# A two-layer attention, mLSTM and HGRN2 block: projections and output tiles beside the mLSTM released in quarters at every step of the recurrence

## The chip, the cores and the metric

The kernel runs on one core of a Trainium2 chip. A core has TensorE (PE in the profile, with PEld for its weight loads), VectorE (DVE), ScalarE (ACT), GpSimd (POOL) and SyncE (SP), which issues most DMAs; POOL issues the others. Each engine takes its own instructions in order and waits on semaphores for the others. The metric is the device time of one execution in microseconds (us), lower is better.

## The reference

1024 latent tokens and 256 context tokens of width 1024 pass through two layers. Layer 0 runs neighbourhood attention (16 heads) and a bidirectional mLSTM (4 heads of width 256) side by side, from one input projection to one output projection. Layer 1 has bidirectional HGRN2 heads. Cut to what matters here:

```python
def _ab_mixer(h_lat, h_ctx, w_in, ...):
    qa, ka, va, za, qb, kb, vb, ob, zb, g = _split_cols(h @ w_in, AB_SIZES)
    oa = neighbourhood_attention(qa, ka, va, ...)        # and context attention
    hb = mlstm forward + mlstm backward (qb, kb, vb, gates)
    hb = _rms(hb * sigmoid(ob), h_norm)
    ya, yb = oa * silu(za), hb * silu(zb)
    return concatenate([ya, yb]) @ w_out

def step(carry, xs):                # one chunk of the mLSTM, per head and direction
    C, n, m = carry
    s = (q k^T) * exp(dmat - m_t)
    num = s v + carry_w * q C ;  den = sum(s) + carry_w * q n
    h = num / max(|den|, exp(-m_t))
    C = dec * C + kw^T v ;       n = dec * n + sum(kw)
```

The output projection of layer 0 is a sum of two halves: `ya @ w_out[:1024]`, which needs the attention alone, and `yb @ w_out[1024:]`, which needs the mLSTM.

## The kernel before

All values are float32. Dense products split each operand into a rounded high part and the rest (`split`, L72 to L75: an ACT cast and a DVE subtraction) and sum three products, hi·hi, hi·lo and lo·hi, so one block of a projection is three matmuls (L127 to L129) and one block of the output projection is three matmuls (L745 to L747).

The token axis is cut into NT = 10 tiles of 128. The mLSTM works on chunks of 128 in both directions. `ml_all` (L424) runs its four heads staggered by five steps: at step g, head h works on its chunk i = g - 5h, where that is 0 to 9, so steps g = 0 to 4 have one head, 5 to 19 two heads and 20 to 24 one head. For each head and each of two directions `ml_rec` (L454) builds a decay matrix on DVE and ACT, multiplies it with the scores to SD (L466), and runs on TensorE the matmul with SD (the SD matmul, L468), two with the carried state C (L478) and two for the update of C (L485), with the C update on DVE (L493). Chunks of q, k and v are loaded one step ahead by SP (`ml_load`, L389, and L421 for q and k), transposed on TensorE (L400, L406) and multiplied to scores (L413). When both directions of a chunk are done, `ml_out` (L516) gates it with the o and z projections (L521 to L528, the root on POOL L152 and L154), transposes it (L532) and stores it. A float32 matmul on these unsplit operands shows as two records of the trace (L468, L478, L485, L413); a transpose shows as one.

Beside the recurrence the kernel has other work for TensorE, here called the filler. It consists of

- the v, o and z projections of head 3 (`ml_ahead`, L307, through `proj_out`, L269): each loads four weight blocks by SP, splits them, and makes five tiles of two token tiles by 256 columns, 48 matmuls each, 256 wide, followed by an eviction on ACT or ACT and DVE and a store from POOL;
- the first half of the output projection (`out_some`, L751): for each of two column blocks b = 1 and b = 0 of 512 columns, eight weight blocks are loaded and split, and for each of the ten token tiles two pieces of the attention's output are loaded (L732) and split (yh, yl), 24 matmuls 512 wide are summed, and the sum is copied by ACT (L756), to the accumulator in SBUF for b = 1 and through POOL's queue to DRAM for b = 0.

The filler's PSUM tiles are in the two banks of the tag "mm". The recurrence uses "tr" (two banks), "s" (two) and "acc" (two), not "mm". After the recurrence the second half of the output projection (`out_tile`, with weights `w2`) uses "mm" again.

The order of instructions on each engine is fixed when the program is built. A planner hands out instructions by priority along a planned timeline; of those that are ready in its plan, the one traced earlier goes first. `filler()` (L300) moves what is traced in it behind everything else by a million places, so the filler runs only where the recurrence has nothing ready in the plan. `issue_after(at)` adds an edge from the matmul `at` to each matmul traced in the block, so none of them stands before `at` in TensorE's order; loads, splits and evictions on other engines get no such edge. Which filler may run from which step is written out by hand in two tables:

```python
ML_AHEAD = {-1: ("v", 3), 1: ("o", 3), 4: ("z", 3)}
ML_OUT = {1: (8, 8, 9, 9, 10, 10, 11, 11, 12, 12), 0: (13, 14, 14, 15, 16, 17, 18, 20, 22, 24)}
```

v of head 3 goes in before the recurrence, behind a matmul of the attention; o after step 1, z after step 4; output tiles of block 1 two at a time after steps 8 to 12, those of block 0 after steps 13 to 24. The edge starts at the last SD matmul of that step. At step 7 the split input (`hh`, `hl`, all that the projections read) is released and the pool "oy" opens in its place, with the accumulator and seven of the slots for output weights; the other four are the projections' weight slots.

Of the kernel before, what the change touches and what calls it, by code (L numbers as in the profile page):

```python
# [9 lines left out]
F32 = mybir.dt.float32  # L10
# [8 lines left out]
P = 128  # L19
D = 1024  # L20
KD = D // P
# [25 lines left out]
class Prog:  # L47
# [81 lines left out]
            mm(ps, lhsT=ll(k), rhs=rh(k), start=False, stop=(last and k == nk - 1))  # L129


    def proj_nat(self, ps, w, tt, c0, n):
        hh, hl = self.hh, self.hl
        s = slice(tt * P, (tt + 1) * P)
        self.dense(
            ps, lambda k: hh[:, k, s], lambda k: hl[:, k, s],
            lambda k: w.h(k)[:, c0 : c0 + n], lambda k: w.l(k)[:, c0 : c0 + n], KD,
        )


# [122 lines left out]


    def na_values(self, b):
        self.proj_out(2 * D + b * 256, self.vd[:, b * 256 : (b + 1) * 256])
# [38 lines left out]


    def ml_ahead(self, part, h, rev=False):  # L307
        c0 = (4 + "qkvoz".index(part)) * D + h * 256
        gate = {"o": self.gate_o, "z": self.gate_z, "q": self.gate_q}.get(part)
        dst = self.md[(part, h)] = self.md_all[len(self.md)]  # L310
        self.proj_out(c0, dst, gate, rev)


    def ml_gates(self, pool, keep):
# [109 lines left out]
    def ml_all(self, pool):  # L424
# [20 lines left out]
        for g in range(5 * 3 + NT):  # L445
            for h in range(4):
                scores = load(h, g + 1 - 5 * h) if 0 <= g + 1 - 5 * h < NT else []
                if 0 <= g - 5 * h < NT:
                    at = self.ml_rec(h, g - 5 * h, seqs, st[h], pool)
                for score in scores:  # L450
                    score()
            yield g, at

    def ml_rec(self, h, i, seqs, st, pool):  # L454
        nc = self.nc
        C, hs = st["C"], st["hs"]
        for d in range(2):
            c = seqs[d][i]
            lastc = P - 1 if d == 0 else 0
# [8 lines left out]
            at = nc.tensor.matmul(num, lhsT=SD, rhs=st["v"][c], start=True, stop=(i == 0))  # L468
            if i > 0 or i < NT - 1:
                cw = self.t(pool, [P, P], F32, "mcw", 4)  # L470
                nc.scalar.activation(cw, Gb, AF.Exp, scale=-1.0, bias=self.mpb[:, d, h, i : i + 1])
# [36 lines left out]
            else:  # L508
# [4 lines left out]
        return at  # L513


    def ml_out(self, h, tt, hs, pool):  # L516
# [219 lines left out]
        return yh, yl  # L736


    def out_sum(self, ps, w, tt, qs, ysrc, yp, bufs, ys=None, rp=None):
        mm = self.nc.tensor.matmul  # L740
        for q in qs:
            yh, yl = ys[q] if ys else self.out_y(tt, q, ysrc, yp, bufs, rp)
            for k in range(8):
                kk = (q - qs[0]) * 8 + k
                mm(ps, lhsT=yh[:, k, :], rhs=w.h(kk), start=(kk == 0), stop=False)  # L745
                mm(ps, lhsT=yh[:, k, :], rhs=w.l(kk), start=False, stop=False)  # L746
                mm(ps, lhsT=yl[:, k, :], rhs=w.h(kk), start=False, stop=(kk == 8 * len(qs) - 1))  # L747
# [462 lines left out]
    def build(self):  # L1210
# [3 lines left out]
        with ExitStack() as es:  # L1214
# [107 lines left out]
                    if p2 < 7:  # L1322
                        z = self.na_z(p2 + 1, pool)
            with tc.tile_pool(name="ml", bufs=2) as pool, self.pp.phase(s=2, acc=2):
                wq, self.six = {}, [(self.wp, "w", 4)] * 4
                with self.filler(), tc.issue_after(self.at[8]):
                    self.ml_ahead(*ML_AHEAD[-1])
                self.mask = self.t(pool, [P, 2, P], F32, "mmask", 1)
                dma(out=self.mask, in_=a["mmask"])

                def wo(q, b, ring=None):
                    if not ring:
                        ring, self.six = self.six[:8], self.six[8:] + self.six[:8]
                    src = a["woab"][q * D : (q + 1) * D, b * 512 : b * 512 + 512]
                    return self.wblock(None, "wo", [src], 8, 512, ring=ring)

                for g, at in self.ml_all(pool):
                    with self.filler(), tc.issue_after(at.ins):
                        if g in ML_AHEAD:
                            self.ml_ahead(*ML_AHEAD[g])  # L1340
                        if g == 7:
                            rh.close()
                            wr, self.ogb = es.enter_context(ExitStack()), 1
                            yp = wr.enter_context(tc.tile_pool(name="oy", bufs=1, side="right"))
                            acc = self.t(yp, [P, NT, 512], F32, "oacc", 1)
                            self.six = self.six + [(yp, "wo", 7)] * 7
# [50 lines left out]
            with l1:  # L1397
# [44 lines left out]
                raw = [pool, 3, "wraw"]  # L1442
                for i, b in enumerate((1, 0)):
                    w = wo(0, b, (ring * 2)[8 * i : 8 * i + 8], raw)
                    self.out_some(w, 0, range(8), self.yd2, yp, acc if b else None, self.part)
# [156 lines left out]
```

## Time and profile before

| | us |
|---|---|
| three runs | 3517.46, 3510.55, 3509.28 |
| median of the runs | 3510.55 |
| the profiled execution, its own time | 3510.13 |
| its span in the profile | 3508.3 |
| 1341 to 1761 in the span (the mLSTM stage, about): TensorE busy | 408.75 of 420 |
| 1761 to 1841 (rest of the output projection): TensorE busy | 78.16 of 80 |

The mean granted clock of TensorE over the execution is 0.995. In rows with several engines, "(x...)" is the number of records that lie in the stretch. A row of a group has the line of the kernel, the engine, the operation, what it writes and reads, its shape and count, then the busy time in us, the mean length of one in ns, and the idle time of the engine just before them with what ended it. In rows of waits, "A <- B" says that A waited and B ended the wait.

### The profile page before, as it was taken

Reading aid. Unit: us, or ns where it says so; the run is one execution under the profiler, and the core shown is the slowest. Engines: PE = TensorE matmul, PEld = TensorE weight load, DVE = VectorE, ACT = ScalarE, POOL = GpSimd, SP = SyncE. Lnnn points to the kernel's source line nnn. Section 1 sums busy time; section 2 is a strip of 40 time slices with the busy share of each in tenths; the row PEclk is TensorE's granted clock in tenths of the full one; section 3 lists DMA queues with packets and bytes.
Section 4 is the critical chain, followed back from the end, with each engine's and each line's share of the span. In section 5 each row is a group of like instructions: output and inputs, shape, how many; then the busy total and the mean of one; then the engine's idle time right before and its main releaser. Section 6 shows DMA issues by size and latency. Waiting matters only on the chain. (4 is left out here: it accounts for less than half of the span.)

```text
span 3508.3 us, 64938 instructions
## 1 busy us (share of the span) xinstructions
PE 3453.9 (98%) x24438; PEld 3146.4 (90%) x24438; DVE 2374.5 (68%) x6009; ACT 1602.3 (46%) x3700; POOL 526.2 (15%) x844
## 2 busy tenths in 40 slices
PE   8999999999999999999999999999999999999999
PEld 5889999999999999988778999989999999999887
DVE  4668856766666654666767766577777767777855
ACT  5532135555445534555547333344444444444442
POOL 3211121222212211211211111000100000010010
PEclk9999999999999999999999999999999999999999
DMA  7552332332323235364484222211211221121346
GB/s 237 168 160 88 115 90 58 91 87 68 84 77 83 83 88 160 121 183 145 124 258 143 100 103 103 82 37 56 61 48 49 61 61 49 52 64 49 116 146 204
DMA packets 374409, 363.91 MB, mean 104 GB/s; under 512 B 30296, under 2 KB 323096, under 8 KB 373968
## 3 DMA queue, kind: packets, MB, share of 16 engines
q1 hardware_dynamic: 330096, 250.34, 24.4%
q0 software_dynamic: 44000, 109.42, 9.1%
q8 instruction: 193, 3.16, 0.4%
q14 instruction: 120, 0.98, 0.1%
HBM read 276.09 MB, written 83.42 MB: 102 GB/s over the span
## 5 line engine op out<-in xcount | busy, mean ns | idle before, releaser
L127 PE MATMUL mm<-wh,hh 128*128 128x256 f32 x2256 | 649.0, 288 | 4.6 <-DVE ev L922 2.7
L128 PE MATMUL mm<-wl,hh 128*128 128x256 f32 x2256 | 649.0, 288 | 1.9 <-DVE wl L75 1.8
L129 PE MATMUL mm<-wh,hl 128*128 128x256 f32 x2256 | 648.5, 288 | 0.0
L129 PE MATMUL mm<-hh,wl 128*128 128x512 f32 (+1 forms) x1344 | 491.5, 366 | 0.0
L127 PE MATMUL mm<-hh,wh 128*128 128x512 f32 (+1 forms) x1344 | 485.1, 361 | 0.0
L128 PE MATMUL mm<-hl,wh 128*128 128x512 f32 (+1 forms) x1344 | 483.6, 360 | 0.0
L127 PEld LDWEIGHTS mm<-wh,hh 128*128 128x128 f32 x2256 | 431.4, 191 | 12.7 <-issue 6.9
L128 PEld LDWEIGHTS mm<-wl,hh 128*128 128x128 f32 x2256 | 431.6, 191 | 7.2 <-DVE wl L75 2.7
L129 PEld LDWEIGHTS mm<-wh,hl 128*128 128x128 f32 x2256 | 431.1, 191 | 3.6 <-issue 0.7
L74 ACT CAST wh<-wraw 128x512 fp32r<-128x512 f32 x290 | 178.2, 620 | 263.1 <-PE mm L128 130.7
L128 PEld LDWEIGHTS mm<-hl,wh 128*128 128x128 f32 x1344 | 254.0, 189 | 32.0
L129 PEld LDWEIGHTS mm<-hh,wl 128*128 128x128 f32 x1344 | 253.9, 189 | 30.5 <-issue 0.2
L127 PEld LDWEIGHTS mm<-hh,wh 128*128 128x128 f32 x1344 | 254.3, 189 | 29.3
L1109 ACT COPY gksel<-gK 128x512 f32<-128x512 f32 x224 | 147.1, 663 | 218.9 <-PE s L1118 197.6
L75 DVE TENSOR_TENSOR wl<-wraw,wh 128x512 fp32r<-128x512 f32 x290 | 196.5, 686 | 51.9 <-ACT wh L74 49.4
L1118 PE MATMUL s<-gQ,gksel 128*128 128x128 f32 x1536 | 199.9, 276 | 0.0
L1118 PEld LDWEIGHTS s<-gQ,gksel 128*128 128x128 f32 x1536 | 192.4, 191 | 6.9
L745 PE MATMUL mm<-woh,yh 128*128 128x512 f32 x412 | 166.7, 405 | 6.7 <-ACT yh L74 6.5
L747 PE MATMUL mm<-woh,yl 128*128 128x512 f32 x412 | 165.3, 402 | 0.5 <-DVE yl L75 0.5
L746 PE MATMUL mm<-wol,yh 128*128 128x512 f32 x412 | 164.0, 399 | 0.0
L74 ACT CAST wh<-b 128x512 fp32r<-128x512 f32 x124 | 77.0, 622 | 187.1 <-PE sa L129 85.3
L1139 DVE TENSOR_TENSOR gQ<-gQ,gT 128x256 f32<-128x256 f32 x384 | 143.2, 414 | 26.1 <-PE s L1118 26.0
(456 smaller groups left out, 8491.9 us busy)
## 6 DMA issues: line engine op xcount, KB each, us to landing
wraw<-yd SPq DMA_DIRECT2D x144, 256.0 KB
wraw<-in_wc_dram SPq DMA_DIRECT2D x128, 256.0 KB
wraw<-in_wab_dram SPq DMA_DIRECT2D x98, 256.0 KB
md<-ev POOLq DMA_DIRECT2D x94, 256.0 KB, 2.8
adar<-in_wada_dram POOLq DMA_DIRECT2D x32, 512.0 KB, 4.9
b<-in_wc_dram SPq DMA_DIRECT2D x64, 256.0 KB
vzd<-qo POOLq DMA_DIRECT2D x56, 256.0 KB, 2.5
adar<-in_wada_dram SPq DMA_DIRECT2D x16, 512.0 KB
```

What stands on the lines that cost most here:

```text
L74: nc.scalar.copy(hi, x)
L75: nc.vector.tensor_tensor(out=lo, in0=x, in1=hi.bitcast(F32), op=ALU.subtract)
L127: mm(ps, lhsT=lh(k), rhs=rh(k), start=(first and k == 0), stop=False)
L128: mm(ps, lhsT=lh(k), rhs=rl(k), start=False, stop=False)
L129: mm(ps, lhsT=ll(k), rhs=rh(k), start=False, stop=(last and k == nk - 1))
L745: mm(ps, lhsT=yh[:, k, :], rhs=w.h(kk), start=(kk == 0), stop=False)
L746: mm(ps, lhsT=yh[:, k, :], rhs=w.l(kk), start=False, stop=False)
L747: mm(ps, lhsT=yl[:, k, :], rhs=w.h(kk), start=False, stop=(kk == 8 * len(qs) - 1))
L1109: nc.scalar.copy(ksel.rearrange("p (b s i) -> p b s i", s=2, i=h), pick(K))
L1118: nc.tensor.matmul(pa[:, c, :].rearrange("p (b s i) -> p b s i", s=2, i=h), lhsT=ksel[:, c * P : (c + 1) * P], rhs=qp[:, c * nbc : (c + 1) ...
L1139: nc.vector.tensor_tensor(out=t[:, i, :, s, :], in0=t[:, i, :, s, :], in1=bc(tot), op=ALU.mult)
```

## The change

The two tables go. `proj_out` and `out_some` become generators that stop after each quarter of a tile: 12 matmuls of a projection tile's 48, or 6 of an output tile's 24; the eviction and the store go with the last quarter. The o and z projections of head 3 and the twenty output tiles form one sequence, `beside()`, of 40 + 80 quarters. `ml_all` now yields after each head of each step, with a rate and its two SD matmuls (one for each direction). For each SD matmul the rate is added to a count, and as many whole quarters as the count holds are taken from the sequence, as filler with an edge from that SD matmul. The rate is 2.0 in steps with one head and 1.4 in steps with two, so the calls offer 20 x 2.0 + 60 x 1.4 = 124 quarters. The release of `hh` and `hl` and the opening of "oy" follow the last quarter of z, wherever that falls. v of head 3 stays where it was. Other users of the two helpers run the generators to their end at once.

```diff
-ML_AHEAD = {-1: ("v", 3), 1: ("o", 3), 4: ("z", 3)}
 ML_ORDER = [8, 9, 4, 5, 6, 7, 0, 1, 2, 3]
-ML_OUT = {1: (8, 8, 9, 9, 10, 10, 11, 11, 12, 12), 0: (13, 14, 14, 15, 16, 17, 18, 20, 22, 24)}
+ML_RATE = (2.0, 1.4)
...
     def proj_out(self, c0, dst, gate=None, rev=False):
...
             for j in range(2):
-                self.proj_nat(ps[:, j, :], w, tt + j, 0, 256)
+                for k in range(0, KD, 4):
+                    self.proj_nat(ps[:, j, :], w, tt + j, 0, 256, k, 4)
+                    if j + k < 5:
+                        yield
...
             nc.gpsimd.dma_start(out=dst[tt * P : (tt + 2) * P, :].rearrange("(j p) f -> p j f", p=P), in_=v)
+            yield
...
                 if 0 <= g - 5 * h < NT:
-                    at = self.ml_rec(h, g - 5 * h, seqs, st[h], pool)
+                    ats = self.ml_rec(h, g - 5 * h, seqs, st[h], pool)
+                    yield ML_RATE[5 <= g < 20], ats
                 for score in scores:
                     score()
-            yield g, at
...
+    def out_part(self, ps, w, y, ks, first, last):
+        mm = self.nc.tensor.matmul
+        yh, yl = y
+        for k, kk in ks:
+            mm(ps, lhsT=yh[:, k, :], rhs=w.h(kk), start=(first and k == 0), stop=False)
+            mm(ps, lhsT=yh[:, k, :], rhs=w.l(kk), start=False, stop=False)
+            mm(ps, lhsT=yl[:, k, :], rhs=w.h(kk), start=False, stop=(last and k == 7))
...
     def out_some(self, w, q, order, ysrc, yp, acc, dst):
         for tt in order:
             ps = self.ps("mm", [P, 512])
-            self.out_sum(ps, w, tt, (q,), ysrc, yp, 2)
+            y = self.out_y(tt, q, ysrc, yp, 2)
+            for k in range(0, 8, 2):
+                self.out_part(ps, w, y, [(k, k), (k + 1, k + 1)], True, True)
+                if k < 6:
+                    yield
             o = self.t(yp, [P, 512], F32, "ox", 2) if acc is None else acc[:, tt, :]
             self.nc.scalar.copy(o, ps)
             if acc is None:
                 self.nc.gpsimd.dma_start(out=dst[tt * P : (tt + 1) * P, 0:512], in_=o)
+            yield
...
-                for g, at in self.ml_all(pool):
-                    with self.filler(), tc.issue_after(at.ins):
-                        if g in ML_AHEAD:
-                            self.ml_ahead(*ML_AHEAD[g])
-                        if g == 7:
-                            rh.close()
...
-                        for b in (1, 0):
-                            if g == ML_OUT[b][0]:
-                                wq[b] = wo(0, b)
-                            for tt in [t for t, at_g in zip(ML_ORDER, ML_OUT[b]) if at_g == g]:
-                                self.out_some(wq[b], 0, [tt], self.yd, yp, acc if b else None, self.x1)
+                def beside():
+                    for part in "oz":
+                        yield from self.ml_parts(part, 3)
+                    rh.close()
...
+                    for b in (1, 0):
+                        yield from self.out_some(wo(0, b), 0, ML_ORDER, self.yd, self.yp, self.acc if b else None, self.x1)
+
+                fill, due = beside(), 0.0
+                for rate, ats in self.ml_all(pool):
+                    for at in ats:
+                        due += rate
+                        with self.filler(), tc.issue_after(at):
+                            while due >= 1.0:
+                                next(fill, None)
+                                due -= 1.0
+                with self.filler():
+                    for _ in fill:
+                        pass
```

More of the change, by code (lines that the diff above doesn't have):

```diff
@@ L135, in proj_nat @@
         self.dense(
-            ps, lambda k: hh[:, k, s], lambda k: hl[:, k, s],
-            lambda k: w.h(k)[:, c0 : c0 + n], lambda k: w.l(k)[:, c0 : c0 + n], KD,
+            ps, lambda k: hh[:, k0 + k, s], lambda k: hl[:, k0 + k, s],
+            lambda k: w.h(k0 + k)[:, c0 : c0 + n], lambda k: w.l(k0 + k)[:, c0 : c0 + n], nk, k0 == 0, k0 + nk == KD,
         )
@@ L265, in na_values @@
     def na_values(self, b):
-        self.proj_out(2 * D + b * 256, self.vd[:, b * 256 : (b + 1) * 256])
+        for _ in self.proj_out(2 * D + b * 256, self.vd[:, b * 256 : (b + 1) * 256]):
+            pass
     def proj_out(self, c0, dst, gate=None, rev=False):
@@ L307, in ml_ahead, with ml_parts @@
     def ml_ahead(self, part, h, rev=False):
+        for _ in self.ml_parts(part, h, rev):
+            pass
+    def ml_parts(self, part, h, rev=False):
         c0 = (4 + "qkvoz".index(part)) * D + h * 256
@@ L310, in ml_ahead @@
         dst = self.md[(part, h)] = self.md_all[len(self.md)]
-        self.proj_out(c0, dst, gate, rev)
+        return self.proj_out(c0, dst, gate, rev)
     def ml_gates(self, pool, keep):
@@ L467, in ml_rec @@
             num = self.ps("acc", [P, 258])
-            at = nc.tensor.matmul(num, lhsT=SD, rhs=st["v"][c], start=True, stop=(i == 0))
+            ats.append(nc.tensor.matmul(num, lhsT=SD, rhs=st["v"][c], start=True, stop=(i == 0)).ins)
             if i > 0 or i < NT - 1:
@@ L512, in ml_rec @@
                 self.ml_out(h, c, hs[c], pool)
-        return at
+        return ats
     def ml_out(self, h, tt, hs, pool):
@@ L736, in out_y @@
         return yh, yl
+    def out_part(self, ps, w, y, ks, first, last):
[5 more added lines that the diff above has]
+            mm(ps, lhsT=yl[:, k, :], rhs=w.h(kk), start=False, stop=(last and k == 7))
     def out_sum(self, ps, w, tt, qs, ysrc, yp, bufs, ys=None, rp=None):
-        mm = self.nc.tensor.matmul
         for q in qs:
[L742 to L747, printed above, removed]
+            y = ys[q] if ys else self.out_y(tt, q, ysrc, yp, bufs, rp)
+            self.out_part(ps, w, y, [(k, (q - qs[0]) * 8 + k) for k in range(8)], q == qs[0], q == qs[-1])
     def out_some(self, w, q, order, ysrc, yp, acc, dst):
@@ L1444, in build @@
                     w = wo(0, b, (ring * 2)[8 * i : 8 * i + 8], raw)
-                    self.out_some(w, 0, range(8), self.yd2, yp, acc if b else None, self.part)
+                    for _ in self.out_some(w, 0, range(8), self.yd2, yp, acc if b else None, self.part):
+                        pass
                 w2 = wo(1, 1, ring[4:], raw)
```

18 lines of the change are left out of this document (10 added, 8 removed).

## The prediction

> **What bounds the kernel now.** I read the page's busy shares first, then stretches of the mLSTM stage of layer 0 (some 420 us, the only part whose order the change touches), then what TensorE waited for there.
>
> ```profile
> PE 3453.9 (98%) x24438; PEld 3146.4 (90%) x24438; DVE 2374.5 (68%) x6009; ACT 1602.3 (46%) x3700; POOL 526.2 (15%) x844
> ```
>
> TensorE sets the time. An unchanged set of matmuls becomes faster only where TensorE stands still. The next views are cut at the starts of steps g = 5, 10, 13, 15 and 20, at the last SD matmul, and in the tail. Each row has the stretch and its length, then busy time and records of PE, PEld, DVE, ACT and POOL, the granted clock, the DMA share and GB/s:
>
> ```profile
> 1414.00:1505.70 91.70, 88.12 (x591) 81.58 (x591) 62.15 (x195) 52.05 (x148) 21.50 (x57) 1.00 0.47 144
> 1505.70:1569.00 63.30, 63.30 (x300) 52.64 (x299) 42.08 (x126) 37.28 (x96) 8.23 (x28) 1.00 0.61 182
> 1569.00:1635.40 66.40, 63.98 (x298) 52.17 (x297) 37.02 (x103) 37.19 (x99) 9.03 (x24) 0.95 0.52 159
> 1635.40:1714.90 79.50, 76.80 (x382) 63.02 (x381) 58.33 (x196) 51.37 (x151) 19.36 (x47) 1.00 0.46 138
> 1714.90:1746.10 31.20, 30.41 (x139) 24.83 (x139) 23.21 (x78) 13.95 (x38) 6.90 (x14) 1.00 0.27 80
> 1746.10:1765.00 18.90, 18.45 (x80) 14.19 (x81) 11.30 (x24) 9.17 (x24) 5.32 (x11) 1.00 0.68 207
> 1765.00:1845.00 80.00, 78.16 (x345) 61.36 (x343) 54.91 (x99) 35.14 (x79) 12.02 (x23) 1.00 0.81 256
> ```
>
> The same stretches with the instructions on the "mm" banks alone (PE, PEld, DVE, ACT). This is the filler, from 1505.7 on all of it 512 wide:
>
> ```profile
> 1505.70:1569.00 63.30, 45.14 (x160) 29.40 (x160) 0.00 (x0) 3.49 (x6) 1.00 0.61 182
> 1569.00:1635.40 66.40, 42.04 (x153) 27.66 (x152) 0.00 (x0) 3.48 (x6) 0.95 0.52 159
> 1635.40:1714.90 79.50, 27.84 (x96) 17.98 (x96) 0.00 (x0) 2.89 (x5) 1.00 0.46 138
> 1714.90:1746.10 31.20, 13.41 (x48) 8.95 (x48) 0.00 (x0) 1.14 (x2) 1.00 0.27 80
> 1746.10:1765.00 18.90, 17.26 (x68) 12.34 (x69) 0.68 (x1) 0.58 (x1) 1.00 0.68 207
> ```
>
> And the SD matmuls (L468), two records each, four of them in a step with two heads; 24, 17 and 40 records are 3, 2 (one record lies over the cut) and 5 steps:
>
> ```profile
> 1505.70:1569.00 63.30, 7.18 (x24) 4.41 (x25) 1.00 0.61 182
> 1569.00:1635.40 66.40, 5.72 (x17) 3.17 (x17) 0.95 0.52 159
> 1635.40:1714.90 79.50, 11.97 (x40) 7.31 (x41) 1.00 0.46 138
> ```
>
> So the filler per step is 160/3 = 53 in g 10 to 12, 153/2 = 77 in g 13 and 14, and 96/5 = 19 in g 15 to 19. At 53 a step TensorE shows no idle time at all. Elsewhere busy time hides short waits, because a matmul's shown length exceeds the distance to the next one. Where it matters I count records times distance. The distances, from rows with start and busy time:
>
> ```profile
> 1698.01 0.40 PE L747 MATMUL mm<-wh,yl 128*128 128x512 f32 x1
> ...
> 1698.94 0.40 PE L745 MATMUL mm<-wh,yh 128*128 128x512 f32 x1
> ...
> 1699.72 0.38 PE L406 MATMUL tr<-ident,mkn 128*128 128x128 f32 x2
> ...
> 1706.83 0.60 PE L468 MATMUL acc<-mv,mSD 128*128 128x258 f32 x2
> 1707.26 1.03 PE L478 MATMUL acc<-mC,mqc 128*128 128x258 f32 x4
> ```
>
> 512 wide: three rows are left out between the first two, so (1698.94 - 1698.01)/4 = 0.23. 258 wide: (1.03 - 0.60)/2 = 0.215. 128 wide: 0.38 less one of 0.28 is 0.10. The records of g 15 to 19 beside the 96:
>
> ```profile
> L485 PE MATMUL s<-mvw,mkn 128*128 128x258 f32 x76 | 22.2, 385 | 0.0
> L478 PE MATMUL acc<-mC,mqc 128*128 128x258 f32 x72 | 19.1, 381 | 0.0
> L468 PE MATMUL acc<-mv,mSD 128*128 128x258 f32 x40 | 12.0, 381 | 0.0
> ...
> L413 PE MATMUL s<-mqT,mkT 128*128 128x128 f32 x40 | 6.5, 284 | 0.4 <-ACT myt L533 0.4
> ...
> L532 PE MATMUL tr<-ident,mhs 128*128 128x128 f32 x20 | 5.6, 283 | 1.0 <-ACT mqT L402 0.5 <-ACT myt L533 0.4
> L406 PE MATMUL tr<-ident,mkn 128*128 128x128 f32 x20 | 4.0, 280 | 0.6 <-ACT mkT L408 0.6
> L400 PE MATMUL tr<-ident,mqn 128*128 128x128 f32 x18 | 3.5, 278 | 0.7 <-ACT myt L533 0.6
> ```
>
> 188 x 0.215 + 98 x 0.10 + 96 x 0.23 = 40.4 + 9.8 + 22.1 = 72.3 of 79.5 us; the rounding of the distances can hide 1 us, so I take **6.0 us lost, 1.2 a step**. In g 13 and 14 the filler run, 160 + 153 = 313, is all thirteen tiles (13 x 24 = 312) that the table had released: TensorE had caught up, and inside g 14 the recurrence stood alone:
>
> ```profile
> 1610.00:1615.00 5.00, 2.62 (x12) 1.81 (x13) 4.07 (x9) 3.19 (x11) 1.36 (x3) 0.87 0.31 95
> 1615.00:1620.00 5.00, 5.00 (x14) 3.85 (x13) 2.29 (x8) 1.81 (x7) 0.72 (x1) 0.50 0.90 300
> ```
>
> TensorE idles 2.4 of 5 us, then its granted clock is 0.50. The mean of 0.95 over 66.4 us makes the clock's share 0.05 x 66.4 = 3.3 us: **5.7 us lost**. What ended the largest waits between 1480 and 1845 us (total, times, longest):
>
> ```profile
> PE tr L400 <- DMA mqn<-md: 2.2, 1, 2.2
> PE tr L406 <- ACT mkT L408: 1.9, 3, 1.3
> PE tr L532 <- DVE mhs L528: 1.7, 2, 1.1
> ```
>
> These are transposes of the recurrence that TensorE, taking its work in order, reached before their input was there. Filler ahead of them gives the input time.
>
> **The change, part by part.** No instruction is added or removed. A quarter is 6 matmuls 512 wide (6 x 0.23 = 1.4 us) or 12 that are half as wide, estimated at the same 1.4. Sums, evictions, stores and loads stay the same in number; what moves is the place from which they may run. The edge to the SD matmul is order on TensorE's own queue, no semaphore. A quarter that stays open holds one of two "mm" banks, which nothing else uses before the recurrence ends, so I cost it at nothing; without that cover the loser waits for the rest of a tile, at most 24 x 0.23 = 5.5 us.
>
> *Steps 0 to 11: 0 us.* In the stretch of g 5 to 9 L127, a third of each projection, has
>
> ```profile
> 1414.00:1505.70 91.70, 32.19 (x103) 19.45 (x103) 1.00 0.47 144
> ```
>
> so 309 matmuls or 26 of the 40 projection quarters run there, 5.2 a step. The new rates release 20 by the end of g 4, where 14 are used, and 1.4 x 4 = 5.6 a step then: the supply stays ahead in both kernels. The hole at the change from z to the output weights (2.2, the mqn row, most of the 3.6 idle in that stretch) comes from a load of the recurrence; both kernels issue the first output weights in g 8, so they pass the recurrence's mqn and mkn loads on SP's queue alike. Between one such wait less and one more, -2.2 to +2.2, I take 0.
>
> *Steps 12 to 19.* By the end of g 12 the rates have released 20 + 8 x 5.6 = 64.8 quarters, 24.8 of them output, 149 matmuls, where before had run 160. From there the supply is the limit: 5.6 x 6 = 34 matmuls a step instead of 77 and later 19. Between the rows of 53 (0 lost) and 19 (1.2), a straight line gives 1.2 - 1.2 x 15/34 = 0.7. Before gave its 19 in one piece behind the last SD matmul of a step; four portions of 8 stand before more of the transposes, so I take 0.5. Seven steps, 13 to 19, cost 3.5 (0 to 8.4 at the two rows' rates). The second block's weights still have to be split on DVE beside the recurrence: I add 1.0 (0 to the 2.4 of idle time in g 14). Before lost 5.7 + 6.0 = 11.7 there, so **-7.2** (-11.7 to -0.9).
>
> *Steps 20 to 24 and the tail.* 24 matmuls a step instead of 48/5 = 10, and the last quarter in g 23 instead of a tile in g 24. Idle there is 0.8 + 0.45, and 1.8 in the tail. The third block's weights find their slots free earlier, but the DMAs are at 0.81 there. Bounds: all 3.0 gone, or one more hole of 2.4 where the end of the recurrence stands bare. I take -0.5.
>
> Sum: 3510.1 (the profiled execution: span 3508.3 and 1.8 us around it) - 7.2 - 0.5 = 3502.4. That execution is 0.4 us under the median of 3510.55, so I forecast **3503**.
>
> **Rivals.**
> *Thin cover trips the clock: slower.* Place: g 13 to 19. The long pieces of before go, and 34 may not stand where the hole is. A step in which the recurrence stands bare as in g 14 costs 2.4 of waits and 3.3 of clock. Three such steps of seven and four at 1.2 are 21.9, less 11.7: +10.2, **3521**. It decides from two: 11.4 + 5 x 1.2 = 17.4 is already 5.7 more than before; seven would be 39.9, +28. For it: steps at 19 lose nearly every time. Against it: those five kept a clock of 1.00, and 34 is more.
>
> [...]
>
> *The order hardly changes.* The filler keeps its low priority. Where the recurrence has nothing ready in the plan, all that is released goes in one piece, and two portions of 8 cover no more than one of 19. Then 1.2 a step stays: 8.4 + 2.4 = 10.8 against 11.7, **3510**. For it: the 19 of before is what two portions are.
>
> *All holes close.* -11.7, the 2.2 of mqn and the 3.0 at the end: -16.9, **3494**. Against it: nothing in the change touches the mqn load.
>
> **How the numbers follow.** Forecast 0.45, its own range 3498 to 3510; hardly any change of order 0.22; thin cover 0.23; all holes 0.10. A difference of 0.3%, 10.5 us, is about what a measurement of this kernel tells from none. Faster by more (under 3500): the last case, 0.20 of the first, 0.03 of the second, together 0.33. Slower by more (over 3521): half of thin cover and somewhat more for its steps beyond three, 0.15, and 0.06 of the second case, whose order may shift the stages behind it: 0.21. Within: 0.46. The range 3494 to 3524 leaves out half of the last case and somewhat under half of thin cover.
>
> **What would show it.** Right: 34 or so filler matmuls in each of g 13 to 19, granted clock 1.00 from 1600 to 1640, under 5 us lost in those seven steps, and steps 0 to 11 within 1 us with the mqn wait still there. Wrong: filler in pieces of 16 or more two to a step; new clock drops; longer L406 and L532 waits; over 3 us of change outside the stage and its tail, which nothing in my sum holds.

## The result, and the profile after

| | before | after |
|---|---|---|
| median of 14 runs, on one chip, us | 3512.29 (3508.71 to 3517.46) | 3504.34 (3500.17 to 3509.35) |
| the profiled execution, us | 3510.13 | 3501.30 |
| its span, us | 3508.3 | 3499.5 |
| mean granted clock | 0.995 | 0.996 |

The ratio after to before is 0.9977, 95% interval [0.9969, 0.9985]: 8 us faster, between 5 and 11. The forecast was 3503. The gain is somewhat under the 0.3% that the prediction had named as about what a measurement tells from none; over 14 runs of each kernel, its interval still lies clear of a ratio of 1.

The page of the kernel after, its first part, with the row that answers to the one of before:

```profile
span 3499.5 us, 64946 instructions
...
PE 3450.0 (99%) x24438; PEld 3146.7 (90%) x24438; DVE 2376.4 (68%) x6009; ACT 1603.3 (46%) x3700; POOL 527.1 (15%) x844
```

The same 24438 matmuls, 98% and then 99% of the span. The span is 8.8 us shorter; TensorE's busy time fell by 3.9 us, and its idle time by the rest. The stretches of the mLSTM stage, cut at the same points of the recurrence as before (starts of g = 5, 10, 13, 15 and 20, the last SD matmul), and then the tail:

```profile
1412.30:1503.80 91.50, 87.92 (x592) 81.64 (x591) 61.81 (x195) 51.97 (x148) 21.30 (x57) 1.00 0.48 144
1503.80:1564.60 60.80, 60.80 (x283) 50.69 (x282) 41.83 (x127) 36.13 (x96) 8.46 (x28) 0.97 0.59 180
1564.60:1607.80 43.20, 42.04 (x216) 34.82 (x215) 27.35 (x85) 27.15 (x79) 7.96 (x22) 1.00 0.47 144
1607.80:1701.30 93.50, 91.58 (x450) 75.95 (x449) 65.45 (x206) 59.06 (x165) 19.89 (x47) 1.00 0.51 152
1701.30:1744.90 43.60, 43.60 (x200) 36.33 (x199) 29.81 (x87) 21.54 (x55) 10.66 (x20) 1.00 0.41 131
1744.90:1845.00 100.10, 98.55 (x444) 78.74 (x443) 71.93 (x139) 48.15 (x114) 17.95 (x34) 1.00 0.78 249
```

Steps 5 to 9 take as long as before (91.5 against 91.7), with the same 3.6 us of idle time. Steps 13 and 14 went from 66.4 us to 43.2 and steps 15 to 19 from 79.5 to 93.5: the filler moved from the former to the latter, as the instructions on "mm" show (third, fourth and fifth stretch):

```profile
1564.60:1607.80 43.20, 22.33 (x71) 12.79 (x70) 0.00 (x0) 1.73 (x3) 1.00 0.47 144
1607.80:1701.30 93.50, 50.71 (x168) 31.08 (x168) 0.00 (x0) 4.05 (x7) 1.00 0.51 152
1701.30:1744.90 43.60, 32.54 (x105) 19.32 (x105) 0.00 (x0) 2.31 (x4) 1.00 0.41 131
```

71/2 = 36 a step, then 168/5 = 34, then 105/5 = 21. What matters is the time lost, so records times distance again, over steps 13 to 19. The groups of the recurrence's matmuls in 1564.6 to 1701.3 (136.7 us, by line and shape):

```profile
L495 PE MATMUL s<-mvw,mkn 128*128 128x258 f32 x106 | 30.9, 382 | 0.0
L488 PE MATMUL acc<-mC,mqc 128*128 128x258 f32 x104 | 27.8, 381 | 0.0
...
L478 PE MATMUL acc<-mv,mSD 128*128 128x258 f32 x56 | 16.9, 383 | 0.0
...
L423 PE MATMUL s<-mqT,mkT 128*128 128x128 f32 x64 | 10.5, 287 | 1.8 <-DVE mC L503 1.7
L542 PE MATMUL tr<-ident,mhs 128*128 128x128 f32 x30 | 8.2, 279 | 0.8 <-ACT myt L543 0.7
L416 PE MATMUL tr<-ident,mkn 128*128 128x128 f32 x32 | 6.2, 275 | 0.5 <-ACT mkT L418 0.5
L410 PE MATMUL tr<-ident,mqn 128*128 128x128 f32 x32 | 6.1, 274 | 0.0
```

For the comparisons from here on I use finer distances, the medians between starts of neighbours without a wait: 0.2155 (258 wide), 0.2295 (512), 0.1085 (128). 266 x 0.2155 + 239 x 0.2295 + 158 x 0.1085 = 57.3 + 54.9 + 17.1 = 129.3 of 136.7 us: 7.4 us lost. Counted step by step, from the first SD matmul of a step to that of the next (filler matmuls, and in brackets the us lost; the row of step 24 runs on to 19 us after the last SD matmul, and "tail" is from there to 100 us after it). The losses of the experiments further down are counted in the same way; the count is good to some 0.2 us.

```
step     before     before again  after
13       75 (0.2)   75 (0.2)      34 (0.6)
14       77 (6.9)   77 (7.8)      36 (2.4)
15       24 (0.1)   24 (0.1)      36 (0.2)
16       18 (0.1)   18 (0.1)      34 (0.2)
17       19 (2.1)   19 (2.3)      30 (0.8)
18       24 (1.2)   24 (1.2)      32 (0.6)
19       11 (3.1)   11 (3.0)      36 (2.8)
13-19      13.7       14.7           7.6
24       68 (2.4)   68 (3.1)      89 (0.8)
tail        4.1        3.8           2.4
20-tail     7.2        7.8           3.6
```

("Before again" is a second profile of the kernel before, experiment 8.) A hole is here a place where TensorE loses a microsecond or more. The gain is the hole of step 14, 4.5 us and more, 1.3 to 1.5 of step 17, some 2 of step 24, and up to 1.7 of the tail, which varies by more than that between kernels. The waits of TensorE in the kernel after, 1480 to 1845 us, show the same:

```profile
PE tr L410 <- DMA mqn<-md: 2.0, 1, 2.0
PE tr L416 <- ACT mkT L418: 2.0, 2, 1.5
PE s L423 <- DVE mC L503: 1.7, 2, 1.3
PE tr L542 <- ACT myt L543: 0.7, 1, 0.7
PE mm L753 <- ACT yh L74: 0.6, 2, 0.4
PE mm L753 <- ACT ox L773: 0.6, 1, 0.6
...
```

L410, L416 and L542 are L400, L406 and L532 of before. The wait of L532 for mhs (1.7 in all) is gone with the hole of step 14. The mqn wait at the change from z to the output weights (the z hole below) is there still. The wait for mC is the 1.3 us that step 19 keeps.

The clock around the place of the old hole, and in the only new drop (at the z hole; same columns as the stretches):

```profile
1498.00:1503.00 5.00, 1.93 (x15) 1.56 (x14) 3.26 (x8) 3.09 (x9) 0.73 (x1) 1.00 0.75 174
1503.00:1508.00 5.00, 4.49 (x17) 3.88 (x18) 3.07 (x10) 3.84 (x11) 0.00 (x0) 0.66 1.09 357
...
1600.00:1640.00 40.00, 39.96 (x194) 33.11 (x194) 29.32 (x94) 26.70 (x69) 3.89 (x13) 1.00 0.54 163
```

From 1600 to 1640, where before had half clock for 6.8 us, the clock is 1.00. The drop at 1504 lasts 3.4 us (0.97 over 60.8 us is 0.03 x 60.8 = 1.8 us lost). It isn't the change's: before again has it too, at 1508.

Outside the stage little moves. The same matmul starts 0.5 us earlier in the trace of after at 1340 us (up to 2.6 earlier before that, at 300 us, in a part that the change does not touch), 9.8 earlier at 1840, and 8.5 or a little more from 1900 to the end.

### The profile page after: what moved, and what is told of

It is laid out like the page before. It is cut to its first block, busy times and chain, and to the rows that moved or that the text cites. A ratio compares the mean times of both kernels' runs of the same rounds, so it can differ in the third digit from the quotient of the medians.

```text
span 3499.5 us, 64946 instructions
## 1 busy us (share of the span) xinstructions
PE 3450.0 (99%) x24438; PEld 3146.7 (90%) x24438; DVE 2376.4 (68%) x6009; ACT 1603.3 (46%) x3700; POOL 527.1 (15%) x844
## 5 line engine op out<-in xcount | busy, mean ns | idle before, releaser
L753 PE MATMUL mm<-woh,yh 128*128 128x512 f32 x412 | 167.8, 407 | 5.5 <-ACT yh L74 5.0
```

Source lines behind the costliest of these rows:

```text
L753: mm(ps, lhsT=yh[:, k, :], rhs=w.h(kk), start=(first and k == 0), stop=False)
```

## The experiments

All but the eighth were timed in five rounds beside the kernel before. Those of one group share their runs of before (median 3513.77 us of 33 runs for 1 to 4, 3513.27 of 25 for 5 to 8, 3513.65 of 24 for 9 to 12). Each is an edit of the kernel after, if nothing else is said. On the same footing after has 0.9977 [0.9969, 0.9985].

The change has two parts, the amounts (even over the steps) and the places (portions behind each SD matmul). Experiments 1 and 2 do one of them each.

**1. Even amounts, in one piece a step**, behind the step's last SD matmul as in before.

```diff
+                    self.ml_last = not 0 <= g - 5 * (h + 1) < NT
...
-                    for at in ats:
-                        due += rate
-                        with self.filler(), tc.issue_after(at):
+                    due += 2 * rate
+                    if rate == 2.0 or self.ml_last:
+                        with self.filler(), tc.issue_after(ats[-1]):
```

> The changed kernel with its amounts per step (quarters at 2.0 and 1.4 per SD matmul), but all quarters of a step released in one piece behind the step's last SD matmul, as before the change. Theory (TensorE loses time where the recurrence stands bare, and it is the even amount over the steps that removes most bare stretches, 5.7 of the forecast 7.2 us; portions within a step are worth 7 x 0.2 = 1.4): about 6 us faster than before, within 2 us of the changed kernel. Rival (the portions within a step do it): at most 2 us faster. In the trace the clock drop near 1613 is gone by the theory.

3507.4 us, 0.9984 [0.9975, 0.9993]: 5.6 us faster than before. Steps 13 to 19 lose 9.9 us; the hole of step 14 is gone (0.3).

**2. The old table's amounts, in portions behind all SD matmuls of a step.**

```diff
-ML_RATE = (2.0, 1.4)
+ML_STEP = {1: 20, 4: 20, 8: 8, 9: 8, 10: 8, 11: 8, 12: 8, 13: 4, 14: 8, 15: 4, 16: 4, 17: 4, 18: 4, 20: 4, 22: 4, 24: 4}
...
                     for at in ats:
-                        due += rate
+                        end = last and at is ats[-1]
+                        due += (1 / 6 if g == 5 and not end else part) * ML_STEP.get(g if end else g - 1, 0)
...
```

> The changed kernel with the old table's amounts per step, each step's quarters released in equal portions: behind that step's last SD matmul and behind the SD matmuls of the next step but its last. Theory (amounts over the steps): the filler is still used up in g 13 and 14, so only the 1.4 us of the portions: 0 to 2 us faster than before. Rival (the portions do it): 6 to 8 us faster.

3510.85 us, 0.9991 [0.9983, 1.0]: 3 us faster, between 0 and 6. Steps 13 to 19 lose 13.5 us, as in before, and step 14 has 6.2 of them. Its stretches of 5 us:

```profile
1611.00:1616.00 5.00, 3.04 (x14) 1.98 (x12) 4.50 (x13) 3.89 (x10) 0.74 (x2) 1.00 0.69 216
1616.00:1621.00 5.00, 4.41 (x15) 3.59 (x16) 1.91 (x7) 3.53 (x12) 1.53 (x3) 0.66 0.82 237
```

The hole of 2 us and the drop of the clock behind it are back as soon as the old amounts are. So the amounts over the steps are the larger part (5.6 without the portions), the portions the smaller (3.2 without the amounts), and 5.6 + 3.2 = 8.8 is about what both give. The two intervals against before overlap; in the same rounds the medians of 1 and 2 lie 3.4 us apart.

**3. Even rate, but whole tiles:** a tile is handed out when four quarters are due, with the count started at 2.

```diff
-                fill, due = beside(), 0.0
+                fill, due = beside(), 2.0
...
-                            while due >= 1.0:
-                                next(fill, None)
-                                due -= 1.0
+                            while due >= 4.0:
+                                for _ in range(4):
+                                    next(fill, None)
+                                due -= 4.0
```

> The changed kernel with whole tiles in place of quarters: a tile is released when four quarters are due, centred on the same even course. Theory: 6 to 8 us faster than before, within 2 us of the changed kernel, since 24 matmuls every second or third SD matmul still leave no step bare. Rival (the division into quarters is what counts): at most 3 us faster.

3514.68 us, 1.0004 [0.9995, 1.0013]: nothing gained. I had expected most of the gain. Steps 13 to 19 lose 18.0 us, more than before, with 4.8 in step 15 (24 filler matmuls) and 3.6 in step 19 (35). Its largest waits of TensorE in these steps, and the hole of step 15:

```profile
PE tr L542 <- ACT mqT L412: 2.5, 2, 1.2
PE s L423 <- ACT mkT L418: 1.8, 2, 1.0
PE s L495 <- DVE mC L503: 1.4, 1, 1.4
```

```profile
1623.00:1628.00 5.00, 3.25 (x11) 1.58 (x9) 4.80 (x13) 4.86 (x12) 0.00 (x0) 0.90 0.60 205
1628.00:1633.00 5.00, 4.48 (x11) 2.69 (x9) 3.97 (x16) 2.31 (x6) 0.12 (x2) 0.50 0.67 179
```

Other waits than those of before, in other steps, and a clock drop of its own at 1627. The longest of these waits, of L495 for mC, starts from the weights of the second output block: ACT waits for a weight load, DVE then splits two blocks, and the C update (L503) that L495 waits for stands behind them in DVE's order:

```profile
1622.55 1.28 ACT L74 CAST woh<-wraw 128x512 fp32r<-128x512 f32 x2 [1.05 <-DMA wraw<-in_woab_dram]
1623.20 1.35 DVE L75 TENSOR_TENSOR wol<-wraw,woh 128x512 fp32r<-128x512 f32 x2 [0.97 <-ACT woh L74]
1624.47 0.48 DVE L503 SCALAR_TENSOR_TENSOR mC<-mC,mcw,s 128x258 f32<-128x258 f32 x1
...
1625.00 1.27 PE L495 MATMUL s<-mvw,mkn 128*128 128x258 f32 x4 [1.41 <-DVE mC L503]
```

The step's one tile had run ahead of this, 24 matmuls between the second and the third of its four SD matmuls. In after, step 15 has as many splits on DVE (10, 6.7 us, against 10 and 6.8 us here) and loses 0.2: there the filler stands behind each of the four.

**4. All filler released at the start.** This takes cover from the end of the stage, to price a bare step.

```diff
-ML_RATE = (2.0, 1.4)
+ML_RATE = (200.0, 200.0)
```

> The changed kernel with all 120 quarters released at the first SD matmul; they keep their low priority and their order. This asks for the price of a bare recurrence. Theory: the filler runs out by g 14 or 15 (480 matmuls at 53 to 77 a step from g 10), the two-headed steps after that stand bare and cost 2.4 to 5.7 us each, so 5 x 2.4 to 5 x 5.7 = 12 to 28 us against 11.7 lost in these stretches before: 0 to 17 us slower than before, with clock drops after 1640. Rival (where the filler stands makes no difference, the planned order hides it): within 3 us of before.

3514.62 us, 1.0006 [0.9998, 1.0015]. Not as expected: the filler lasted to step 18, at 48 to 101 matmuls a step in steps 13 to 18. From step 9 to 13 it ran as in before, although all of it was released, so it was not the release that held it back. Steps 20 to 23 then stood bare. Their stretch with the start of step 24 as its end, all instructions, and then those on "mm":

```profile
1739.45:1757.94 18.49, 18.06 (x84) 14.94 (x83) 17.16 (x67) 9.89 (x31) 3.92 (x9) 1.00 0.17 50
```

```profile
1739.45:1757.94 18.49, 0.00 (x0) 0.00 (x0) 0.00 (x0) 0.00 (x0) 1.00 0.17 50
```

With no filler at all TensorE idles 0.4 of 18.5 us, and by records times distance the bare steps 20 to 23, with one head each, lose 0.1 or less three times and 1.0 once. The bare step 19, with two heads, loses 4.6. What the early filler saved (steps 13 to 19 lose 6.7, the least of all kernels) came back in the tail, which loses 12.5 us. The tail's waits, and two of its stretches:

```profile
PE mm L753 <- ACT yh L74: 8.0, 5, 4.5
PE mm L755 <- DVE yl L75: 1.4, 1, 1.4
```

```profile
1790.00:1810.00 20.00, 16.22 (x69) 12.48 (x68) 13.20 (x24) 6.52 (x11) 1.93 (x4) 1.00 0.88 288
1810.00:1830.00 20.00, 15.40 (x57) 11.72 (x57) 11.68 (x18) 7.75 (x13) 1.82 (x4) 0.83 0.77 255
```

The second half of the output projection waits for its split inputs, with the DMA engines at 0.88 and 0.77: 3.8 and 4.6 us idle, and a clock of 0.83 for 20 us (3.4 us). That the loads of these inputs now crowd into the tail is how I read it; which load was late was not followed.

**5 and 6. Where in a step.** After experiment 3 my idea was that a step has one stretch, behind the first head's second SD matmul, that wants some 30 filler matmuls, and that the rest wants little. 5 puts all of a step's 5.6 quarters there, 6 puts 3.5 there and 0.7 behind each of the other three.

```diff
-ML_RATE = (2.0, 1.4)
+ML_PART = (0.0, 5.6, 0.0, 0.0)
...
```

(6: `(0.7, 3.5, 0.7, 0.7)`; the steps with one head keep 2.0 for each.)

> The changed kernel with the same 5.6 quarters for each two-headed step, all of them behind the second SD matmul of the first of the two heads (the recurrence's work up to the second head's first SD matmul, 4 to 6 us on TensorE with most of a step's transposes, follows there). New theory after the first four runs: the losses of g 11 to 23 sit in just that stretch (1 to 2 us each with under 30 filler matmuls in it, 0.24 with 30 or more), so the place of the filler counts and not its even course: the loss in g 13 to 19 falls from 7.6 us to 2 to 6, in all 10 to 13 us faster than before. Rival (it is the even course over the SD matmuls, portions small and everywhere): no better than the one piece behind the step's end, 3 to 7 us faster than before.

> As the run before, but 3.5 of the 5.6 quarters (21 matmuls) behind the second SD matmul of the first head and 0.7 (4) behind each of the other three. New theory, if 30 matmuls are the threshold: 1 to 1.5 us lost in each such stretch, g 13 to 19 lose 7 to 10 us, 6 to 8 us faster than before, not better than the changed kernel. If the loss falls steadily with the filler in the stretch: 3 to 6 us lost, 9 to 12 us faster than before. Rival (even course): 3 to 7 us faster.

5: 3504.16 us, 0.9976 [0.9966, 0.9985]; steps 13 to 19 lose 7.3. 6: 3506.06 us, 0.9982 [0.9973, 0.9991]; 9.1. Neither beats after, and the idea falls: with 30, 22 and 30 matmuls in the place in question, steps 14, 16 and 17 of 5 still lose 1.7, 1.8 and 2.0. The holes moved (step 19 from 2.8 to 1.2), their sum did not. Experiment 5 shows one thing more: in steps 5 to 19, the 30 to 36 matmuls of a step released behind one of its four SD matmuls gain as much as four portions, where the same amounts behind the last one (experiment 1) gained 5.6. Portions are not needed if the one piece stands in a good place.

**7. Three buffers for mqn instead of two.** The mqn wait of 2.0 at the z hole is the longest one left.

```diff
-        q = self.ml_qk("q", h, tt, pool, "mqn", 2)
+        q = self.ml_qk("q", h, tt, pool, "mqn", 3)
```

> The changed kernel with three buffers instead of two for the loaded q chunks (mqn). It asks whether the hole in g 9 and 10, at the change from z to the output weights (5.9 us lost there in the changed kernel, a wait of 2.0 us for mqn in it), comes from the mqn load being held back. Theory (it is): 2 to 4 us less lost there, 10 to 12 us faster than before. Rival (the hole is the time that the first output weights and yd pieces take to land and be split, and the recurrence is bare meanwhile): 5 to 7 us still lost there, 8 us faster than before as the changed kernel.

3504.69 us, 0.9974 [0.9965, 0.9983], as after. TensorE's waits from 1478 to 1522, all there are, first of after and then of 7:

```profile
PE tr L410 <- DMA mqn<-md: 2.0, 1, 2.0
PE tr L416 <- ACT mkT L418: 1.5, 1, 1.5
```

```profile
PE tr L416 <- ACT mkT L418: 4.0, 2, 2.3
```

The mqn wait is gone and the next transposes wait instead, for their bank to be copied out by ACT: 3.5 us of waits before, 4.0 now. The longer of the two is again a wait for a load. The copy (L418) stands in ACT's order behind the cast of an output weight block, and that cast waits 2.75 us for its DMA:

```profile
1504.60 0.62 ACT L74 CAST woh<-wraw 128x512 fp32r<-128x512 f32 x1 [2.75 <-DMA wraw<-in_woab_dram]
...
1505.58 0.36 ACT L418 COPY mkT<-tr 128x256 f32<-128x256 f32 x1
...
1505.99 0.44 PE L416 MATMUL tr<-ident,mkn 128*128 128x128 f32 x2 [2.32 <-ACT mkT L418]
```

So the rival of this run, that the hole is the time in which the first output weights land and are split, has the trace on its side, though no run moved these loads. By records times distance steps 9 and 10 together lose 4.7 us instead of 5.9, where 2 to 4 less were expected by the theory; two profiles of before differ there by as much (experiment 8).

**8. The kernel before again**, unchanged, for one more profile, to see what of the differences is the order's and what one execution's.

> The kernel before once more, for a second profile of the same program: how far two profiles differ by themselves. In the first profile g 0 lost 1.5 us (a wait for mqn), and none of the five kernels since has that. If the changed order removes it, it is here again; if it was one late load of that execution, it is gone here and the stretch from step 0 to the end of the tail differs by under 1 us besides.

Its one run took 3515.72 us. The 1.5 us that the first profile loses in step 0 (1.3 of them a wait for an mqn load) are not there, so that was one late load and not the order. The hole of step 14 is there, with 7.8 us, and the clock falls behind it again:

```profile
1612.00:1617.00 5.00, 3.27 (x15) 1.85 (x13) 3.49 (x12) 2.37 (x8) 1.23 (x4) 1.00 0.57 181
1617.00:1624.00 7.00, 5.87 (x15) 4.48 (x16) 4.15 (x12) 3.80 (x13) 1.60 (x3) 0.53 0.76 231
```

Two profiles of one order agree within 0.9 us in every one of the steps 13 to 24; the first hole in steps 9 and 10 varies by 1.3 together.

**9 and 10. An amount for each step.** In before, steps 15 and 16 lose nothing at 18 to 24 matmuls, and steps 14 and 19 lose most. 9 takes filler from the former for the latter; 10 is 9 with the edit of 7.

```diff
-ML_RATE = (2.0, 1.4)
+ML_STEP = (4.0, 4.0, 4.0, 4.0, 4.0, 5.6, 5.6, 5.6, 5.6, 5.6, 5.6, 5.6, 6, 7, 10, 3, 3, 7, 7, 9.8, 1, 1, 1, 2, 3)
...
-                    yield ML_RATE[5 <= g < 20], ats
+                    yield ML_STEP[g] / (4 if 5 <= g < 20 else 2), ats
```

> The changed kernel with other amounts per step, evenly over the SD matmuls of a step: as before to g 11, then 6, 7, 10, 3, 3, 7, 7 and 9.8 quarters in g 12 to 19 and 1, 1, 1, 2, 3 in g 20 to 24 (the changed kernel: 5.6 and 4). Steps 14 and 19, where one head's last chunks and the next head's first loads meet, lost most (2.4 and 2.8 us in the changed kernel), steps 15, 16 and 20 to 23 next to nothing at any amount. Theory (the filler covers the recurrence's waits, and steps differ in what they need): g 13 to 19 lose 3 to 5 us instead of 7.6, 10 to 12 us faster than before. Rival (what is left there no longer depends on the amount): 7 to 9 us faster, as the changed kernel. If g 20 to 24 need their 4 quarters after all: under 6.

> The run before with three buffers for the q chunks, which took 1 us off g 9 and 10 in its own run. If the two add: 11 to 13 us faster than before; if not: 8 to 10.

9: 3504.46 us, 0.9974 [0.9963, 0.9984]. Steps 15 to 18 lose some 1.0 us together at 18 to 38 matmuls and step 19, at 66, loses 1.3 instead of 2.8. But step 14 loses 2.8 at 72, and step 13 loses 2.2 at the 34 at which it lost 0.6 in after; 13 to 19 come to 7.2. 10: 3504.6 us, 0.9978 [0.9969, 0.9987]; what step 9 gains by the third mqn buffer (4.5 to 1.9 us lost), step 10 gives back (1.5 to 4.5). Amounts as uneven as 18 to 72 a step thus gain what even ones do, so evenness as such is not what pays.

**11 and 12. Size or place of the pieces.** 3 changed both: whole tiles, and other places for them. 11 hands out halves (count started at 1), 12 whole tiles again, two quarters later than in 3.

```diff
-                fill, due = beside(), 0.0
+                fill, due = beside(), 1.0
...
-                            while due >= 1.0:
-                                next(fill, None)
-                                due -= 1.0
+                            while due >= 2.0:
+                                for _ in range(2):
+                                    next(fill, None)
+                                due -= 2.0
```

(12: the count starts at 0.0, with the loop of experiment 3.)

> The changed kernel with half tiles (12 matmuls 512 wide) released when two quarters are due, centred on the same course. Whole tiles gave no gain at all (+1.4 us), quarters 8. Theory of size (each SD matmul needs its portion, and larger pieces leave bare stretches between): between the two, 2 to 6 us faster than before. Rival (whole tiles lost by where they happened to fall, not by their size): 6 to 9 us faster.

> The whole tiles of e3, each released two quarters later on the even course, so that they fall behind other SD matmuls. Theory of size: no gain again, 2 us slower to 3 faster than before, and two-headed steps with clock drops or holes of 2 us and more where no tile stands. Rival (the place they fell on): 4 to 8 us faster than before.

11: 3503.62 us, 0.9971 [0.996, 0.9983]; steps 13 to 19 lose 7.0. 12: 3510.56 us, 0.9995 [0.9986, 1.0004]; 12.9, with 4.1 in step 16, the steps having between 19 and 48 matmuls. Whole tiles gain nothing that can be told from zero in either place, and halves gain what quarters do. The length of a piece is not what decides: experiment 5 releases 30 to 36 matmuls in one piece and gains all. What whole tiles change with it is the amount of a step (24 to 47 in experiment 3, 19 to 48 here, as a tile falls into it or not) and the place; which of these costs the gain was not tried apart. No version beats after beyond its interval.

## Why the prediction held

**The time.** 3503 was forecast, 3504.3 is the median. The sum was made against a profiled execution of 3510.1, and before's median over 14 runs is 3512.3, so the forecast change was -7.7 of that execution and the measured one is -8.0 (3504.34 - 3512.29) of the medians. That they agree to 0.3 us is in part luck: the measured change is known to some 3 us either way, and two terms below were each wrong by more than that 0.3.

**Steps 0 to 11: 0 us.** Right. Steps 1 to 8 lose 0.1 us or less each in all kernels, and the mqn wait stayed (2.2, then 2.0). Two differences between the profiles cancel here and are not the change's, as experiment 8 shows: the 1.5 us of step 0 in before, and some 1.5 in step 10 in after, where the clock dropped. Experiment 7 took the mqn wait away, and the next wait took its place: 1.2 us less were lost, inside the bounds of -2.2 to +2.2.

**Steps 12 to 19: -7.2.** Right within 1 us, by two terms that were both too small. The forecast was 11.7 lost before and 4.5 after; the finer count gives 13.7 (14.7 in the second profile) and 7.6, thus -6.1 to -7.1. That the two errors, 2.0 to 3.0 and 3.1, cancel in the difference is luck. The loss that was left was 1.1 a step (7.6/7) where 0.5 and the 1.0 for the weights had been put. "Under 5 us lost in those seven steps" was missed for that. The weights' own 1.0 was not what was short: in after, DVE splits them in steps 15 and 16, which lose 0.2 each. "34 or so in each" was right (30 to 36), and so was the clock of 1.00 from 1600 to 1640.

The term that was mis-sized is the straight line of loss by filler, 0 at 53 and 1.2 at 19. There is no such line. Steps 15 and 16 lose 0.1 each at 18 to 24 in before, steps 14 and 19 lose 2.4 and 2.8 at 36 in after, and step 14 still 2.8 at 72 in experiment 9. The five steps whose 1.2 I had taken as a mean were 0.1, 0.1, 2.1, 1.2 and 3.1. Steps 14 and 19 are those in which one head takes its last step and the next head's first loads come, but the loss does not belong to the step either: in experiment 1 these two lose 0.3 and 0.5 (at 53 each), and in 3 and 12 the worst are step 15 (4.8 at 24) and step 16 (4.1 at 24), which lost 0.1 in before at about the same amount.

**Portions stand before more of the transposes.** Shown in part: experiment 2, with portions alone, gains 3.2 us (0 to 6), and experiment 1, without them, 2 to 3 less than after, though their intervals overlap. Experiment 5 narrows it: one piece a step in another place does as well, so the place counts and not the division.

**A half-open quarter costs nothing.** Nothing contradicts it: the only wait for a bank of "mm" in after, that of L753 for the copy to ox, is 0.6 us, once. The wait of up to 5.5 us for the rest of a tile, put down for the case that something else needs the bank, shows in no run. Whole tiles (experiments 3 and 12) cost the gain, but none of the waits of TensorE in their steps 13 to 19 is one for a bank of "mm".

**Steps 20 to 24 and the tail: -0.5.** Too small. 7.2 (7.8) went to 3.6. The hole of step 24 (2.4, 3.1) fell to 0.8, as the filler ends in step 23 or 24 in quarters and not with a whole tile. In the tail (4.1 and 3.8 to 2.4) the same stretch takes 1.9 to 6.1 us of loss in kernels that differ only in earlier steps, experiment 4 apart, so I don't count it to the change.

**The rivals.** "Thin cover trips the clock" had a price of 5.7 us for a bare step. Experiment 4 measured it: 4.6 for a bare step of two heads, and 0 to 1.0 for each of the four with one head, all at a clock of 1.00. In after none of the seven steps has a drop (1.00 from 1564.6 to 1701.3), but in experiment 3 a drop follows the thin cover of step 15 (24 matmuls, 4.8 us lost; clock 0.50 from 1628 to 1633), so what the rival feared does happen. "The order hardly changes" falls: 153 filler matmuls in steps 13 and 14 became 71. "All holes close" didn't happen: the loads it needed were not touched, and in experiments 5, 6, 7, 9 and 10 other holes opened where one was closed, with 7 to 9 us left over the seven steps each time.

What stays open is which wait sets those 7 us. The longest ones differ from kernel to kernel (for mC in after, for mkT in 9 and 11). One thing the traces have in common: in every kernel that loses over 9 us in steps 13 to 19, the step that loses most is one in which DVE splits weights of the second output block (step 14 in before and experiment 2, 15 in 3 and 6, 16 in 1 and 12). Steps 15 of after and 11 have six or seven of these eight splits and lose 0.2, so the splits alone do not do it; that a step with splits needs its filler in the right places is argued from these rows, and no run moved the splits alone.

## What to carry to other kernels

Filler beside an in-order recurrence should not be used up before the steps that need it. Here quarters and halves of a tile at an even rate gained 8 to 10 us, and so did uneven amounts in quarters and one piece of 30 to 36 matmuls a step in a good place; whole tiles at the even rate, which give some steps one and others two, gained nothing, and finer than a half bought nothing. Count the loss of each step (its length less records times distance) before spreading cover evenly or drawing a line through means: the same step lost 0.3 us in one order and 6.9 in another, and not by its amount of filler. And when the longest wait is removed, look up what waits next and what that waits for: in experiment 7 a bank's copy took the place of a load, and the copy itself stood behind a cast that waited for another load.

## What the runs showed of the hardware

In the mLSTM stage of before and after the clock fell behind pauses of TensorE of 2.04 us and less. In before the drop begins at 1613.7, and in the 5 us ahead of it TensorE was idle for 2.01, in pieces of 0.57, 0.63 and 1.14 us, the last of which runs on into the drop:

```profile
1608.70:1613.70 5.00, 2.99 (x15) 1.92 (x13) 3.52 (x11) 2.92 (x9) 1.48 (x4) 1.00 0.46 147
1613.70:1620.50 6.80, 6.39 (x16) 4.89 (x17) 3.43 (x11) 3.61 (x14) 1.37 (x3) 0.50 0.73 242
```

In after there are two pieces, 1.54 and 2.04 us, as these rows of the timeline show (start, length, instruction, and in brackets the idle time before it and what ended it), with the clock in the stretches behind them. The first piece ends 4.4 us ahead of the drop, the second 0.5:

```profile
1499.64 0.44 PE L416 MATMUL tr<-ident,mkn 128*128 128x128 f32 x2 [1.54 <-ACT mkT L418]
...
1503.51 0.41 PE L410 MATMUL tr<-ident,mqn 128*128 128x128 f32 x2 [2.04 <-DMA mqn<-md]
```

```profile
1504.00:1507.40 3.40, 3.40 (x13) 2.86 (x12) 2.47 (x6) 3.32 (x9) 0.00 (x0) 0.52 1.08 360
1507.40:1511.40 4.00, 4.00 (x19) 3.36 (x18) 3.23 (x13) 3.73 (x9) 0.00 (x0) 0.98 0.98 290
```

Half clock lasted 3.4 us in after (from 1504; 1.7 us lost) and 6.8 in before (from 1613.7; 3.4 lost). Idle time that was spread out went without a drop: step 19 of experiment 4 idles 2.4 us in 17.8 and keeps 1.00:

```profile
1721.63:1739.45 17.82, 15.44 (x80) 11.61 (x79) 11.84 (x42) 11.29 (x36) 3.37 (x7) 1.00 0.39 116
```

How much idle time is enough was not found. At the z hole of before, in its first profile, TensorE was idle for 2.93 of 5 us, with a last piece of 2.19, and no drop follows:

```profile
1505.48 0.41 PE L400 MATMUL tr<-ident,mqn 128*128 128x128 f32 x2 [2.19 <-DMA mqn<-md]
```

```profile
1500.50:1505.50 5.00, 2.07 (x15) 1.63 (x15) 2.67 (x7) 2.27 (x8) 0.72 (x1) 1.00 0.75 200
1505.50:1512.30 6.80, 6.80 (x34) 5.64 (x35) 5.19 (x17) 5.94 (x16) 0.00 (x0) 1.00 1.12 351
```

One order gave a drop in one execution and none in another: the second profile of before has one behind the z hole, at 1508 (its mean clock over the execution is 0.994, that of the first 0.995).
